# Where a tile starts in SBUF: widening four small tiles so that all large tiles start at the same residue modulo 256 bytes

## The chip, the cores and the metric

The kernel runs on one core of one Trainium2 chip. The metric is the device time of one execution in microseconds (us). The time before is 1183.08 us, the median of 3 runs (1182.72 to 1183.48). In what follows PE is the matrix engine (TensorE), PEld its weight loads, DVE the vector engine, ACT the scalar engine, POOL GpSimd, SP the queue that issues most DMAs.

## The reference

One decoder layer over a sequence of 1024 tokens of width 1024, all in float32: a gated linear recurrence (HGRN2) with 8 heads of 128, an output projection, and an MLP with a squared ReLU of hidden width 4096, each behind an RMSNorm.

```python
h = _rmsnorm(x, norm_mix)
q, f, i, g = split(h @ w_in, 4)                      # (1024 x 1024) @ (1024 x 4096)
log_f = logaddexp(log(lb), log1p(-lb) + log_sigmoid(f));  k = (1 - lb) * sigmoid(-f)
S_t = diag(f_t) S_{t-1} + k_t v_t^T;  o_t = S_t^T q_t     # per head, in chunks
mix = (rms(o) * out_norm * silu(g)) @ w_out
x = x + mix
a = relu(_rmsnorm(x, norm_mlp) @ w1)                 # 1024 x 4096
x = x + (a * a) @ w2
out = _rmsnorm(x, norm_final)
```

## The kernel before

Every large product is done in a split form: an operand is kept as a rounded part and a remainder (`t[:, 0]` and `t[:, 1]`, or two tiles `h` and `l`), and `split_mm` (lines 206 to 209) issues three matmuls for a product of 128 x 128 by 128 x 512: high by high (L207), high by low (L208), low by high (L209). The third argument after the weights is the moving operand, of 512 columns; the weights of 128 columns are loaded by PEld while the matmul before runs. There are 4,464 such matmuls. On top of that the products go by a Strassen-like scheme of 7 block products for 8, whose sums of blocks are `t1` to `t4` on the side of the activations and `s1` to `s4` on the side of the weights.

The stages on PE, by the profile's names for their results, with matmuls of 512 columns:

| stage | from, to (us) | moving operand | weights | matmuls |
|---|---|---|---|---|
| `pp`: first head, unsplit | 14, 72 | `h0B` | `w0`, `w1` | 192 |
| `pX`, `pY`, `pZ`: 7 heads, beside the scan's small matmuls | 72, 438 | `h0B` and `t4`, or `t1` to `t3` | `w2` to `w15` | 1176, 504 of them on `t1` to `t3` |
| `op`: output projection | 438, 549 | `wo` | `zh` | 384 |
| `pl`: first MLP block, unsplit | 549, 597 | `h1B` | `wa0` to `wd0` | 192 |
| `m1X`, `m1Y`, `m1Z`: rest of `h @ w1`, 49 products of 24 | 597, 868 | `h1B` and `t4`, or `t1` to `t3` | 5 pairs of slots in turn | 1176 |
| `m2X`, `m2Y`, `m2Z`: `(a*a) @ w2`, 56 products of 24 | 868, 1176 | the same 5 pairs of slots | 5 pairs of activation slots in turn | 1344 |

(In the profile `t1` to `t4` are all called `ht`.) In `m2` the roles are turned round: the activations are the weights of the matmul, and `w2` moves.

The order on PE is the program's own, and so it is on the other engines but for some of the work between the stages. While PE works on one product, ACT and DVE split the operands of a later one (L775 and L776 the weights, L944 and L945 the activations, L111 and L112 the sums `t`), and SP loads and stores the blocks.

SBUF is given out by pools. The pool `keep` (line 51) grows from the bottom: the identity, `gn`, `mk`, `neghalf` (line 67), then the slots `m0` to `m3`, then small tiles (`lb`, line 258, and others), then the slots `m4` to `m11` and the 16 slots `hT`, then small tiles again (`fs`, line 997, 12 buffers). The pools `scan` (to about 500 us) and `mlp` (after it) stand behind it. The pool `right` (line 53) grows down from the top and holds the 12 slots `d0` to `d11`. A tile takes its columns times 4 bytes in each partition, rounded up to 32. Nearly all slots are of 4,096 bytes, so within a run of slots all start at the same residue modulo 256, and which one is decided by the small tiles ahead of them:

| slots | start modulo 256 | what lies there |
|---|---|---|
| `m0` to `m3` | 32 | raw `w_in`, raw `w_out`; in `m1` and `m2` one of the 5 pairs of weight slots (`m2`, `m3`) and one of the 5 pairs of activation slots |
| `m4` to `m11`, `hT` | 192 | weights of `pp` and `p`; the other 4 pairs of weight slots; `h0B`, `h1B`, `t4`, `zh`, raw `w2` |
| pools `scan`, `mlp` | 128 | the scan's `q`, `k`, `f`, `v`; MLP results `e`, `t`; the other 4 pairs of activation slots |
| `d0` to `d11` | 224 | `x`, `t1` to `t3`, `wo`, `acc`, outputs |

Of the kernel before, what the change touches and what calls it, by code (L numbers as in the profile page):

```python
# [21 lines left out]
F32 = mybir.dt.float32  # L22
# [7 lines left out]
P = 128  # L30
# [18 lines left out]
def trunk(ctx: ExitStack, tc: tile.TileContext, x, gains, masks, gfin, w_in, w_out, w1, w2, out):  # L49
    nc = tc.nc  # L50
    pool = ctx.enter_context(tc.tile_pool(name="keep", bufs=1))
    dram = ctx.enter_context(tc.tile_pool(name="dram", bufs=1, space=bass.MemoryType.DRAM))
    dp = ctx.enter_context(tc.tile_pool(name="right", bufs=1, side="right"))
# [10 lines left out]
    make_identity(nc, ident)  # L64
    gn = pool.tile([P, 4, 8], F32, name="gn")
    mk = pool.tile([P, 8, LEAF], U8, name="mk")
    neghalf = pool.tile([P, 8], F32, name="neghalf")
    nc.gpsimd.memset(neghalf, -0.5)


# [4 lines left out]
    def hslot(half, kb, name):  # L75
        return pool.tile([P, 2, 512], F32R, name=name, tag=f"hT{half}{kb}")

    def dslot(i, shape, name, dt=F32):
        return dp.tile(shape, dt, name=name, tag=f"d{i}")
# [22 lines left out]
    def split_sum(n):  # L102
        half, k0 = SUMS[n]
        for kb in range(4):
            r = R[half, k0 + kb // 2][:, kb % 2]
            if n == "t4":
                t = hslot(1, kb, f"ht4{kb}")
            else:
                t = dslot(("t1", "t2", "t3").index(n) * 4 + kb, [P, 2, 512], f"h{n}{kb}", F32R)
            hc[n, kb] = t  # L110
            nc.scalar.activation(t[:, 0], r, AF.Copy)  # L111
            nc.vector.tensor_tensor(t[:, 1], r, t[:, 0].bitcast(F32), ALU.subtract)  # L112
# [132 lines left out]
    with tc.tile_pool(name="scan", bufs=1) as sp:  # L245
# [9 lines left out]
        Ac = sp.tile([P, NC, LEAF], F32, name="Ac")  # L255


        lb = pool.tile([P, 8], F32, name="lb")
        lo = pool.tile([P, 8], F32, name="lbe")
        nc.vector.tensor_tensor(lb, gn[:, 3, :], gn[:, 3, :], ALU.subtract)  # L260
        nc.scalar.activation(lb, lb, AF.Exp)
# [23 lines left out]
        def value(half, k):  # L285

            shape, name = [P, 2, 512], f"R{half}{k}"
            if (half, k) in ((0, 0), (0, 1), (1, 0)):
                return dslot(8 + 2 * half + k, shape, name)
            tag = {(1, 1): "AT", (0, 2): "kt", (0, 3): "S", (1, 2): "oz", (1, 3): "v"}[half, k]  # L290
            return sp.tile(shape, F32, name=name, tag=tag)
# [87 lines left out]
        def plain_pair(h, tl, j, half):  # L379

            for r in range(2):
                p_ = psum.tile([P, 512], F32, name=f"pp{h}{j}{half}{r}", tag="d")
                for k in range(2):
                    w = weight(2 * h + j, "abcd"[2 * r + k])
                    for kb in range(4):
                        hook()
                        t = hc[BLOCKS[half][k], kb]
                        c = slice(kb * P, (kb + 1) * P)
                        split_mm(p_, w[:, 0, c], w[:, 1, c], t[:, 0], t[:, 1], (k, kb) == (0, 0), (k, kb) == (1, 3))
                        if kb == 2 or (j, half, r, k) == (0, 0, 0, 0):  # L390
                            i = index[2 * h + j, "abcd"[2 * r + k]]
                            ensure(min(i + 3, 4 * PLAIN) if half == 0 else i + 4)
                        pump(650.0)
                if (j, r) == (0, 0):
                    q_part(h, tl, 512 * half, p_)
                elif j == 0:
                    f_half(h, tl, half, p_, 1.0)
                    f_bound(h, tl["f"][:, HALF[half]])
                elif r == 0:
                    tiles(h, tl, "vT")  # L400
                    nc.scalar.activation(tl["vT"][:, HALF[half]], p_, AF.Copy)
                else:
                    g_half(h, tl, half, p_, 1.0)
# [56 lines left out]
        def scan_units(h, tl):  # L460
# [60 lines left out]
            def leaf(m, i):  # L521
                def run():
# [8 lines left out]
                    if m == LEAF // 2:  # L531
                        for b in range(P // LEAF):
                            r = slice(b * LEAF, (b + 1) * LEAF)
                            nc.scalar.activation(AT[r, :, r], Ac[r, :, :], AF.Copy)  # L534
                return run
# [12 lines left out]
            def big(m):  # L548
                def run():
# [8 lines left out]
                    for s0 in range(0, P, 2 * m):  # L558
                        for par in range(2):
                            nc.scalar.activation(AT[s0:s0 + m, par::2, s0 + m:s0 + 2 * m],  # L560
                                                 ps[s0 + m * par:s0 + m * (par + 1)], AF.Copy)
# [42 lines left out]
            def o_unit():  # L604
# [4 lines left out]
                for g in range(2):  # L609
                    ps = psum.tile([P, 4, P], F32, name=f"o{h}{g}", tag="s")  # L610
                    st["o"].append(ps)
                    for j in range(4):
                        c = 4 * g + j
                        nc.tensor.matmul(ps[:, j, :], AT[:, c, :], v[:, c, :], start=True, stop=c == 0)  # L614
                        if c:
# [38 lines left out]
        block_sums()  # L654
        for n in ("t1", "t3", "t2"):
            split_sum(n)
        AT = sp.tile([P, NC, P], F32, name="AT", tag="AT")
        nc.gpsimd.memset(AT, 0.0)
        plain_pair(0, tl, 0, 1)
# [334 lines left out]
        nc.sync.dma_start(t, x1[tb])  # L994

    def fs(name):
        return pool.tile([P, 1], F32, name=name, tag="fs", bufs=12)

    def out_tile(tb):
        return dp.tile([P, D], F32, name=f"ot{tb}", tag=f"d{9 + tb % 3}")  # L1000
# [6 lines left out]
    def rows_out(tb):  # L1007
        ot, ss = out_tile(tb), fs(f"fs{tb}")
        nc.scalar.activation(ot, acc[tb], AF.Square, scale=D ** -0.5, accum_out=ss)  # L1009
        r = rstd_of(ss, EPS, 1, f"f{tb}")  # L1010
        nc.vector.scalar_tensor_tensor(ot, acc[tb], r[:, 0:1], gf, op0=ALU.mult, op1=ALU.mult)
        nc.sync.dma_start(out[tb * P:(tb + 1) * P, :], ot)

    def rows_first_half(tb):

        ot, ss = out_tile(tb), fs(f"fs{tb}")
        nc.scalar.activation(ot[:, :512], acc[tb][:, :512], AF.Square, scale=D ** -0.5, accum_out=ss)
        nc.gpsimd.tensor_scalar(ss, ss, EPS, None, op0=ALU.add)
        nc.vector.tensor_tensor(acc[tb][:, :512], acc[tb][:, :512], gf[:, :512], ALU.mult)
        small[tb] = ss  # L1020

    def rows_second_half(tb):
        ot, ss = out_tile(tb), fs(f"ft{tb}")
        nc.scalar.activation(ot[:, 512:], acc[tb][:, 512:], AF.Square, scale=D ** -0.5, accum_out=ss)
        r = fs(f"fr{tb}")
        nc.gpsimd.tensor_tensor(r, ss, small[tb], ALU.add)
        nc.gpsimd.tensor_tensor(r, r, neghalf[:, :1], ALU.pow)
        rows = slice(tb * P, (tb + 1) * P)
        nc.scalar.activation(ot[:, :512], acc[tb][:, :512], AF.Copy, scale=r[:, 0:1])
        nc.scalar.dma_start(out[rows, :512], ot[:, :512])  # L1030
        nc.vector.scalar_tensor_tensor(ot[:, 512:], acc[tb][:, 512:], r[:, 0:1], gf[:, 512:],
                                       op0=ALU.mult, op1=ALU.mult)
        nc.sync.dma_start(out[rows, 512:], ot[:, 512:])
# [109 lines left out]
```

## Time and profile before

| | before |
|---|---|
| median of 3 runs | 1183.08 us |
| the profiled execution, its own time | 1184.61 us |
| its span (first to last instruction) | 1182.8 us |
| mean granted PE clock | 0.991 |
| PE busy, share of the span | 1157.9 us, 98% |
| DVE, ACT, POOL busy | 797.6, 569.8, 70.7 us |
| DMA | 143.38 MB, mean 121 GB/s |

A busy PE says little by itself: a matmul of 512 columns is shown with about 390 ns, and the next one starts some 227 to 236 ns after it, so neighbours overlap. How fast PE goes is read from the starts: so many matmuls between two starts in the timeline.

### The profile page before, as it was taken

What the parts mean: (1) busy time and instruction counts of PE and PEld (TensorE: products, weight loads), DVE (VectorE), ACT (ScalarE), POOL (GpSimd) and SP (SyncE); (2) the same over time, 40 slices, a digit from 0 to 9 for tenths busy, and PEclk for the clock granted to TensorE, in tenths of its full rate; (3) what the DMA queues carried; (4) which work ended last, traced back from release to release, by engine and by line L of the source; (5) the groups of instructions that cost most, each with busy time, mean ns of one, the idle gap of its engine ahead of it and who ended that gap; (6) DMA issues with size and microseconds to landing.
All of it is one profiled execution on the core that took longest, in us unless ns stands there. A gap on an engine that the chain in (4) does not pass through costs nothing.

```text
span 1182.8 us, 17554 instructions
## 1 busy us (share of the span) xinstructions
PE 1157.9 (98%) x7108; PEld 947.9 (80%) x7108; DVE 797.6 (67%) x1131; ACT 569.8 (48%) x999; POOL 70.7 (6%) x94
## 2 busy tenths in 40 slices
PE   8989999999999999999999999999999999999997
PEld 7777788887878777888888888888888888888886
DVE  5897868787787867425846545654578756677663
ACT  7446455564645564236645444444453443323552
POOL 7500000000000000010000000000000000000011
PEclk9899999999999998999999999999999999999999
DMA  6111111111112175021245234523797544422331
GB/s 254 36 37 37 55 57 64 43 54 55 37 55 71 37 234 194 19 89 71 89 160 192 86 132 178 196 108 111 274 343 303 182 174 155 157 98 90 125 125 72
DMA packets 43138, 143.38 MB, mean 121 GB/s; under 512 B 4912, under 2 KB 5040, under 8 KB 43056
## 3 DMA queue, kind: packets, MB, share of 16 engines
q1 hardware_dynamic: 42192, 141.05, 33.7%
q8 instruction: 56, 0.92, 0.3%
q10 hardware_dynamic: 864, 1.20, 0.3%
q14 instruction: 26, 0.21, 0.1%
HBM read 100.81 MB, written 41.42 MB: 120 GB/s over the span
## 4 chain that ended last, share of the span: by engine, by line
PE 86%; DVE 8%; DMA 2%; POOL 2%; ACT 1%; issue 1%; SPq 0%; POOLq 0%; DVEq 0%; ACTq 0%
PE m2X L207 5%; PE m2X L209 5%; PE m2X L208 5%; PE m1X L207 4%; PE m1X L208 4%; PE m1X L209 4%; PE pX L207 3%; PE pX L208 3%; PE pX L209 3%; PE op L207 3%; PE op L208 2%; PE op L209 2%; PE m2Y L207 2%; PE m2Y L209 2%; PE m2Y L208 2%; PE m1Y L207 2%
## 5 line engine op out<-in xcount | busy, mean ns | idle before, releaser
L944 ACT ACTIVATE a<-ai 128x1024 fp32r<-128x1024 f32 x56 | 59.0, 1054 | 74.5 <-PE m2X L208 25.1
L945 DVE TENSOR_TENSOR a<-ai,a 128x1024 fp32r<-128x1024 f32 x56 | 68.3, 1219 | 11.8 <-ACT a L944 11.8
L847 ACT ACTIVATE e<-e 128x1024 f32<-128x1024 f32 x21 | 22.3, 1062 | 67.8 <-DVE e L978 67.8
L207 PE MATMUL op<-wo,zh 128*128 128x512 f32 x128 | 52.4, 409 | 0.0
L208 PE MATMUL op<-wo,zh 128*128 128x512 f32 x128 | 51.2, 400 | 0.0
L209 PE MATMUL op<-wo,zh 128*128 128x512 f32 x128 | 51.2, 400 | 0.0
L147 DVE TENSOR_TENSOR xr<-xr,op 128x512 f32<-128x512 f32 x24 | 16.5, 688 | 46.5 <-PE op L209 46.3
L1005 DVE TENSOR_TENSOR acc<-acc,m2X 128x512 f32<-128x512 f32 x32 | 21.2, 685 | 37.2 <-PE m2X L209 37.1
L321 DVE TENSOR_TENSOR q<-q,f 128x512 f32<-128x512 f32 x56 | 38.6, 689 | 3.8 <-PE lv L557 2.1
L328 DVE TENSOR_TENSOR k<-k,f 128x512 f32<-128x512 f32 x56 | 38.4, 686 | 0.1
L121 POOL TENSOR_SCALAR rs_f<-fs 128x1 f32<-128x1 f32 x4 | 2.1, 518 | 585.2 <-ACT ot L1009 585.2
L844 ACT ACTIVATE e<-e 128x1024 f32<-128x1024 f32 x32 | 34.0, 1062 | 1.0
L534 ACT ACTIVATE AT<-Ac 32x256 f32<-32x256 f32 x32 | 13.3, 415 | 33.7 <-DVE Ac L530 33.4
L147 DVE TENSOR_TENSOR raw<-raw,raw 128x512 f32<-128x512 f32 x42 | 28.9, 689 | 0.7
L209 PEld LDWEIGHTS op<-wo,zh 128*128 128x128 f32 x128 | 24.4, 191 | 6.0
L207 PEld LDWEIGHTS op<-wo,zh 128*128 128x128 f32 x128 | 24.5, 192 | 5.8
L208 PEld LDWEIGHTS op<-wo,zh 128*128 128x128 f32 x128 | 24.5, 191 | 5.5
L966 ACT ACTIVATE e<-m1X 128x512 f32<-128x512 f32 x28 | 16.0, 592 | 23.8 <-PE m1X L209 23.8
L121 POOL TENSOR_SCALAR rs_z<-zs 128x8 f32<-128x8 f32 x8 | 1.9, 243 | 402.3 <-ACT z L620 402.3
L300 POOL TENSOR_TENSOR R<-h0B 128x512 f32<-128x512 f32 x16 | 25.5, 1627 | 6.4 <-DVE h0B L297 6.4
L626 ACT ACTIVATE z<-o,rs_z 128x128 f32<-128x128 f32 x64 | 17.4, 384 | 16.4 <-POOL rs_z L122 16.4
L614 PE MATMUL o<-v,AT 128*128 128x128 f32 x128 | 23.4, 275 | 0.0
(1720 smaller groups left out, 3766.4 us busy)
## 6 DMA issues: line engine op xcount, KB each, us to landing
raw<-in_w_in SPq DMA_DIRECT2D x32, 512.0 KB, 3.7
ai<-adt SPq DMA_DIRECT2D x32, 512.0 KB, 4.3
adB<-e SPq DMA_DIRECT2D x24, 512.0 KB, 2.6
adt<-t SPq DMA_DIRECT2D x24, 512.0 KB, 4.6
ai<-adB SPq DMA_DIRECT2D x24, 512.0 KB, 4.5
x<-in_x SPq DMA_DIRECT2D x8, 512.0 KB, 7.3
xr<-in_x SPq DMA_DIRECT2D x8, 512.0 KB, 5.4
iw<-in_w_out SPq DMA_DIRECT2D x16, 256.0 KB, 3.4
```

Of the source, the lines that this page charges most:

```text
L147: nc.vector.tensor_tensor(out_, a, b, ALU.add)
L207: nc.tensor.matmul(ps, lhi, rhi, start=start, stop=False, **more)
L208: nc.tensor.matmul(ps, lhi, rlo, start=False, stop=False, **more)
L209: nc.tensor.matmul(ps, llo, rhi, start=False, stop=stop, **more)
L300: nc.gpsimd.tensor_tensor(R[half, kb // 2][:, kb % 2], t[:, 0].bitcast(F32), t[:, 1].bitcast(F32), ALU.add)
L321: nc.vector.tensor_tensor(qo, qo, te.to_broadcast([P, n, m]), ALU.mult)
L328: nc.vector.tensor_tensor(ke, ke, to.to_broadcast([P, n, m]), ALU.mult)
L614: nc.tensor.matmul(ps[:, j, :], AT[:, c, :], v[:, c, :], start=True, stop=c == 0)
L844: nc.scalar.activation(t, t, AF.Square)
L847: nc.scalar.activation(t, t, AF.Relu, scale=sign)
L944: nc.scalar.activation(hi, x, AF.Copy)
L945: nc.vector.tensor_tensor(lo, x, hi.bitcast(F32), ALU.subtract)
```

## The change

Three small tiles get wider or more buffers, and one that nothing reads or writes is added:

- `neghalf` from 8 to 48 columns (32 to 192 bytes): all that follows in `keep` moves up by 160 bytes, `m0` to `m3` from residue 32 to 192.
- `lb` from 8 to 32 columns, of which the first 8 are used (32 to 128 bytes): what follows moves up by 256 bytes in all, so `m4` to `m11` and `hT` stay at 192.
- `fs` from 12 to 14 buffers (64 bytes more): `scan` and `mlp` move up by 320 bytes in all, from 128 to 192.
- `edge`, 32 bytes in `right`: `d0` to `d11` move down by 32 bytes, from 224 to 192.

So every slot of 4 KB starts at 192 modulo 256, and so do the larger ones and those of 2,048 and 3,584 bytes. The program's instructions are the same on every engine and stand in the same order; the one that differs is the memset of `neghalf` on POOL, 48 columns for 8.

```diff
-    neghalf = pool.tile([P, 8], F32, name="neghalf")
+    neghalf = pool.tile([P, 48], F32, name="neghalf")
     nc.gpsimd.memset(neghalf, -0.5)
...
-        lb = pool.tile([P, 8], F32, name="lb")
+        lb = pool.tile([P, 32], F32, name="lb")[:, :8]
...
         for n in ("t1", "t3", "t2"):
             split_sum(n)
+        dp.tile([P, 8], F32, name="edge")
         AT = sp.tile([P, NC, P], F32, name="AT", tag="AT")
...
     def fs(name):
-        return pool.tile([P, 1], F32, name=name, tag="fs", bufs=12)
+        return pool.tile([P, 1], F32, name=name, tag="fs", bufs=14)
```

## Rows read from the trace of the kernel before

**Rows 1.** The page, part 1: busy us (share of the span) xinstructions.

```profile
PE 1157.9 (98%) x7108; PEld 947.9 (80%) x7108; DVE 797.6 (67%) x1131; ACT 569.8 (48%) x999; POOL 70.7 (6%) x94
```

**Rows 2.** The page, part 4: the chain that ended last, by engine.

```profile
PE 86%; DVE 8%; DMA 2%; POOL 2%; ACT 1%; issue 1%; SPq 0%; POOLq 0%; DVEq 0%; ACTq 0%
```

**Rows 3.** Busy time by stage: length, busy us (x instructions), PE clock, DMA share, GB/s.

```profile
72.00:438.00 366.00, 359.20 (x3361) 294.72 (x3350) 286.37 (x547) 198.95 (x493) 13.40 (x14) 1.00 0.20 64
438.00:549.00 111.00, 106.61 (x662) 86.81 (x661) 55.25 (x100) 40.31 (x87) 7.71 (x16) 0.97 0.29 102
597.00:868.00 271.00, 271.00 (x1177) 220.49 (x1176) 150.19 (x148) 132.01 (x158) 0.00 (x0) 1.00 0.44 167
868.00:1176.00 308.00, 307.86 (x1345) 252.07 (x1343) 214.05 (x213) 122.42 (x137) 10.18 (x18) 1.00 0.46 164
```

**Rows 4.** Timeline, PE, first matmuls of products: start us, us, engine, line, out<-moving,weights.

```profile
585.74 0.39 PE L207 MATMUL pl<-h1B,wc0h 128*128 128x512 f32 x1
...
602.06 0.40 PE L207 MATMUL m1Y<-ht,ws11h 128*128 128x512 f32 x1
...
607.66 0.39 PE L207 MATMUL m1X<-ht,ws21h 128*128 128x512 f32 x1
...
613.26 0.40 PE L207 MATMUL m1Y<-h1B,ws41h 128*128 128x512 f32 x1
```

**Rows 5.** Timeline, PE: two products that move `t4`, by two weight slots.

```profile
784.99 0.39 PE L207 MATMUL m1X<-ht,wd5h 128*128 128x512 f32 x1
...
790.43 0.39 PE L207 MATMUL m1X<-h1B,wa6h 128*128 128x512 f32 x1
...
823.63 0.39 PE L207 MATMUL m1X<-ht,wd6h 128*128 128x512 f32 x1
...
829.24 0.39 PE L207 MATMUL m1X<-h1B,wa7h 128*128 128x512 f32 x1
```

**Rows 6.** Timeline, PE: first and last of `m2`, and products in it.

```profile
867.88 0.39 PE L207 MATMUL m2X<-va0sh,a 128*128 128x512 f32 x1
...
1128.45 0.39 PE L208 MATMUL m2X<-vs37sl,a 128*128 128x512 f32 x1
...
1131.62 0.39 PE L207 MATMUL m2Z<-vb4sh,a 128*128 128x512 f32 x1
...
1142.62 0.39 PE L207 MATMUL m2Z<-vb6sh,a 128*128 128x512 f32 x1
...
1175.46 0.40 PE L209 MATMUL m2X<-vd7sh,a 128*128 128x512 f32 x1
```

**Rows 7.** Timeline, PE: a stretch of `op` without other work, and the wait in it.

```profile
445.51 1.51 PE L509 MATMUL lv<-qe,k 128*32 128x48 f32 x64 [4.38 <-ACT qe L502]
...
500.58 0.39 PE L207 MATMUL op<-wo,zh 128*128 128x512 f32 x1
...
528.58 0.39 PE L207 MATMUL op<-wo,zh 128*128 128x512 f32 x1
```

**Rows 8.** Timeline, PE: two products of the heads' stage.

```profile
120.59 0.39 PE L207 MATMUL pX<-ht,w3s 128*128 128x512 f32 x1
...
123.39 0.39 PE L207 MATMUL pY<-h0B,w3s 128*128 128x512 f32 x1
...
127.59 0.40 PE L207 MATMUL pX<-ht,w3d 128*128 128x512 f32 x1
...
130.32 0.39 PE L207 MATMUL pX<-h0B,w4a 128*128 128x512 f32 x1
```

**Rows 9.** Groups of elementwise work: shapes xcount | busy us, mean ns | idle before.

```profile
L147 DVE TENSOR_TENSOR vc<-vc,va 128x1024 f32<-128x1024 f32 x8 | 9.8, 1219 | 0.0
L856 DVE TENSOR_TENSOR t<-e,e 128x1024 f32<-128x1024 f32 x8 | 9.7, 1219 | 0.0
```

**Rows 10.** Timeline, ACT and DVE: the split of the weights `ws21`.

```profile
591.60 1.06 ACT L775 ACTIVATE ws21h<-uc 128x1024 fp32r<-128x1024 f32 x1 [2.55 <-DVE uc L147]
...
592.70 1.23 DVE L776 TENSOR_TENSOR ws21l<-uc,ws21h 128x1024 fp32r<-128x1024 f32 x1 [1.13 <-ACT ws21h L775]
```

## The prediction

> **What bounds the kernel now.** I read the page's busy times and its chain first: PE is busy for 98% of the span and holds 86% of the chain that ended last, DVE 8%, DMA 2% [rows 1, 2]. Then the stages: from 597 to 1176 us PE is busy without a gap (271.00 of 271.00 and 307.86 of 308.00 us), in the heads' stage it idles for 6.8 us of 366 and in the output projection for 4.4 of 111 [rows 3]. So in the MLP the time is the number of matmuls times the distance of their starts, and nothing else; before it this holds nearly, with waits between.
>
> That distance is no constant, and it goes by where the operands lie. I set the timeline's starts beside the table of residues:
>
> - moving operand and weights both at 192: 72 matmuls from 585.74 to 602.06, 16.32 us, 226.7 ns each [rows 4];
> - moving at 224 (`t1`, `t2`): 24 in 5.60 us, 233.3 ns, with the weights at 32 (`ws11`, from 602.06) as at 192 (`ws21`, from 607.66) [rows 4];
> - the same tile `t4` at 192 moving, in one place against weights at 192, in the other against weights at 32: 5.44 and 5.61 us for 24, or 226.7 and 233.8 ns [rows 5]. Stage, engines at work and moving operand are the same; the weight slot alone differs. This pair convinces me most;
> - in `m2`, moving at 192 and weights at 128: 48 from 1131.62 to 1142.62, 11.00 us, 229.2 ns [rows 6];
> - in `m2`, both at 32: the last 14 of a product, from 1128.45 to 1131.62, take 3.17 us, 226.4 ns [rows 6];
> - moving `wo` at 224, weights at 192: 120 in 28.00 us, 233.3 ns [rows 7].
>
> Equal residues run at 226.7 ns, whichever they are; unequal ones at 229 or 233 to 234.
>
> **The change, part by part.** It moves no instruction. It makes the residue of every operand 192, so each class above should go to the first one. I take 226.7 ns (5.44 us for a product of 24) as the pace after, and count stage by stage.
>
> `m2`: 1344 matmuls from 867.88 to 1175.46 us, that is 1343 distances in 307.58 us [rows 6]. At 226.67 ns they are 304.42 us: 3.16 us less. Against it: after a change of class the pace needs some ten matmuls to settle (the product at 32 reached its pace only in its last 14). With one class there is nothing to settle, but the stops of other kinds remain; I take 2.7. Bounds 0 (rival 4) and 3.16; for a loss see rival 3.
>
> `m1`: 49 products from 596.6 us (585.74 and 48 matmuls of `pl` at 226.7 ns) [rows 4, 6] to 867.88, so 271.3 us; 49 x 5.44 is 266.6. That is 4.7 us less, nearly all of it from 26 slow products (21 that move `t1` to `t3`, and 5 more with the weight slot at 32) at 0.16 to 0.17 us each. I take 4.4; bounds 0.8 (the 5 products alone) and 4.7.
>
> `pl`: two products of 24 have their weights at 32, 0.17 us each: 0.3 us.
>
> `op`: 384 matmuls, some 350 of them running free at 233.3 ns. 350 x 6.6 ns is 2.3 us. The stage also holds a wait of 4.38 us for data that the last head's scan and a DMA bring [rows 7]; what PE gains ahead of such a wait is given back in it. I take 2.0; bounds 0 and 2.3.
>
> Heads' stage: 42 products of 12 move `t1` to `t3` at 2.80 us, against 2.73 us for one that moves `t4` [rows 8]. The difference is 0.07 us, so 2.9 us in all. Here not everything is on PE's path: PE waits 6.8 us in all [rows 3], for the scan's DVE work, and DVE is busy 286 of 366 us, so a part of a faster PE turns into longer waits. I take half, 1.5; bounds 0 and 2.9.
>
> `pp`: all at 192 already, nothing.
>
> Elementwise work: a DVE addition of 1,024 columns takes 1219 ns with its tiles at 192 and 1219 ns with them at 128 [rows 9]. So DVE gains and loses nothing by the residue, and the cover it needs (it is busy 364 of the MLP's 579 us) is not touched. The longer memset of `neghalf` is 40 columns more, on POOL, long before the first use: nothing. The DMAs move the same bytes to the same slots, behind a PE that is the bound: nothing. If PE is 3% faster within a product, the splits for the next ones must be ready 0.17 us sooner; with DVE idle for a third of the MLP and PE waiting nowhere in it, I expect no new wait.
>
> Sum: 2.7 + 4.4 + 0.3 + 2.0 + 1.5 = 10.9 us. The profiled execution took 1184.61 us, 1.8 of it outside the span of 1182.8; the gain is all within the span, so 1173.7 for that execution, and from the median of 1183.08 I forecast **1172.2 us**.
>
> [...]
>
> **The rivals.**
>
> 1. *The upper pool is slow, not the residue.* All operands at 224 lie in `right`, at the top of SBUF, so place and residue can't be told apart for `t1` to `t3` and `wo`. If the place decides, `op` and the heads' stage gain nothing and `m1` only its 5 products: 0.8 + 2.7 + 0.3 = 3.8 us, 1179.3 us. For it: no tile in `right` has another residue. Against it: the slot at 32 lies low, among fast ones, and is as slow (233.8 against 233.3).
>
> 2. *The starts don't matter as such.* The weight slot at 32 is slow for another reason that the move does not cure (its distance to the moving tile in larger steps), and so is 224: 1183.1 us. Against it: the same slot at 32 is fast once the other operand is at 32 too [rows 6].
>
> 3. *Equal residues are fast only while the other engines keep away; slower.* After the change ACT, DVE and the DMAs work at 192 as well, where most of theirs now lies at 128 in the MLP. If each of their accesses at PE's residue costs PE its settled pace, the matmuls of `m1` and `m2` fall to 233.8 ns: 2519 x 0.2338 is 588.9 us for today's 578.9, 10 us more, and with half a microsecond from each stage ahead about 1194 us. It decides from a mean of 229.8 ns in the MLP, which is today's (578.9 us over 2519). Against it: while ACT and DVE write `ws21` into slots at 192 [rows 10], PE goes through the 72 matmuls at 226.7 ns without a flaw.
>
> 4. *`m2` doesn't settle.* The products with both at 32 spent their first ten matmuls at about 232 ns. If that is not the change of class but the way `m2` alternates two moving tiles, `m2` keeps its 229 ns: 1172.2 + 2.7 = 1174.9 us.
>
> **How the numbers follow.** The forecast has 0.62, rival 4 0.14, rival 1 0.11, rival 2 0.08, rival 3 0.05. All upper bounds together are 3.16 + 4.7 + 0.3 + 2.3 + 2.9 = 13.4 us, or 1169.7; I set the low end at 1169.5. The forecast's own lower end, with nothing from the heads' stage and half of `m2`, is about 8 us, 1175; to leave out no more than 2 in 10 the range goes on to rival 1's neighbourhood, 1179.5. A change of under 0.2% (2.4 us) can't be told from none in this kernel. Faster by more than that: the forecast, rival 4 and nearly all of rival 1, 0.86. Within it: rival 2 and the rest of rival 1, 0.09. Slower: 0.05.
>
> **What would show it.** In the profile after, a product of `m1` that moves `t1` takes 5.44 us and no longer 5.60, one with the weights in slots `m2` and `m3` the same, `m2` lasts 304 to 305 us, `op` shows 226.7 ns in its free stretch, and the waits in the heads' stage grow by about as much as is missing there. DVE's 1219 ns stays. The forecast is wrong if `t1` keeps 233 ns at 192 (rival 1), if `m2` stays at 229 (rival 4), if the products with slots `m2` and `m3` stay slow (rival 2), or if those that were settled at 226.7 ns lose that pace (rival 3).

## The result, and the profile after

The changed kernel takes **1172.06 us** (median of 6 runs, 1170.51 to 1175.24) against 1183.17 (6 runs, 1182.72 to 1183.53): a ratio of 0.9905, 95% interval 0.9894 to 0.9916. The profiled execution took 1173.07 us with a span of 1171.2, against 1184.61 and 1182.8. Two lines went in, so line numbers after are one or two higher (the matmuls are at L208 to L210).

The page after, part 1 (busy us), the chain by engine, and two rows of part 6 (KB, us to landing):

```profile
PE 1145.7 (98%) x7108; PEld 948.1 (81%) x7108; DVE 796.5 (68%) x1131; ACT 569.1 (49%) x999; POOL 68.5 (6%) x94
...
PE 85%; DVE 8%; DMA 2%; ACT 2%; POOL 1%; issue 1%; SPq 0%; POOLq 0%; DVEq 0%; ACTq 0%
...
ai<-adt SPq DMA_DIRECT2D x32, 512.0 KB, 4.4
...
va<-in_w SPq DMA_DIRECT2D x8, 512.0 KB, 6.1
```

The instructions are as many as in [rows 1]; PE is busy for 12.2 us less, the other engines for about the same. The bound has not moved: PE is at 98% as before and holds nearly the same share of the chain [rows 2]. Busy time by stage after, with the columns of [rows 3]:

```profile
72.00:437.00 365.00, 358.14 (x3331) 295.44 (x3331) 286.10 (x547) 198.00 (x492) 13.38 (x14) 1.00 0.21 65
437.00:545.00 108.00, 102.72 (x652) 85.23 (x651) 54.72 (x100) 39.41 (x86) 7.69 (x16) 0.97 0.29 102
593.00:859.00 266.00, 266.00 (x1176) 220.24 (x1175) 149.50 (x147) 131.33 (x157) 0.00 (x0) 1.00 0.45 169
859.00:1165.00 306.00, 305.25 (x1347) 252.44 (x1345) 214.70 (x213) 122.84 (x138) 8.39 (x18) 1.00 0.47 167
```

In `m1` PE goes through 1176 matmuls in 266.00 us where it had 1177 in 271.00, still without a gap and at the same granted clock of 1.00. In `m2` the last 0.75 us of the window is past the last matmul. PE is not freed of a wait; it goes faster. The timeline of PE after shows where (start us, us, line, out<-moving,weights):

```profile
119.60 0.39 PE L208 MATMUL pX<-ht,w3s 128*128 128x512 f32 x1
...
122.32 0.39 PE L208 MATMUL pY<-h0B,w3s 128*128 128x512 f32 x1
...
443.88 1.51 PE L510 MATMUL lv<-qe,k 128*32 128x48 f32 x64 [5.28 <-ACT qe L503]
...
495.54 0.39 PE L208 MATMUL op<-wo,zh 128*128 128x512 f32 x1
...
522.74 0.39 PE L208 MATMUL op<-wo,zh 128*128 128x512 f32 x1
...
582.01 0.39 PE L208 MATMUL pl<-h1B,wc0h 128*128 128x512 f32 x1
...
598.33 0.39 PE L208 MATMUL m1Y<-ht,ws11h 128*128 128x512 f32 x1
...
603.77 0.39 PE L208 MATMUL m1X<-ht,ws21h 128*128 128x512 f32 x1
...
609.21 0.39 PE L208 MATMUL m1Y<-h1B,ws41h 128*128 128x512 f32 x1
...
815.93 0.39 PE L208 MATMUL m1X<-ht,wd6h 128*128 128x512 f32 x1
...
821.37 0.39 PE L208 MATMUL m1X<-h1B,wa7h 128*128 128x512 f32 x1
...
859.45 0.39 PE L208 MATMUL m2X<-va0sh,a 128*128 128x512 f32 x1
...
1118.07 0.39 PE L209 MATMUL m2X<-vs37sl,a 128*128 128x512 f32 x1
...
1120.57 0.39 PE L208 MATMUL m2Z<-vb4sh,a 128*128 128x512 f32 x1
...
1131.45 0.39 PE L208 MATMUL m2Z<-vb6sh,a 128*128 128x512 f32 x1
...
1163.86 0.39 PE L210 MATMUL m2X<-vd7sh,a 128*128 128x512 f32 x1
```

- The 72 matmuls from 582.01 that were fast before are as fast: 16.32 us [rows 4].
- `ws11` and `ws21`, which move `t1` and `t2` from the upper pool, take 5.44 us each, no longer 5.60 [rows 4].
- `t4` against `wd6`, whose slot has moved from 32 to 192, takes 5.44 us, no longer 5.61 [rows 5].
- `m2`: 1343 distances from 859.45 to 1163.86 are 304.41 us, 226.67 ns each, for 307.58 [rows 6]; 48 from 1120.57 take 10.88 us for 11.00.
- The free stretch of `op`: 120 in 27.20 us for 28.00, but the wait ahead of `lv` is 5.28 us for 4.38 [rows 7].
- A product of twelve with `t1` in the heads' stage: 2.72 us for 2.80 [rows 8].

Of the 2520 matmuls of `m1` and `m2` not one starts other than 226 or 227 ns after its forerunner. The products that the prediction had settling over ten matmuls settle no more, since nothing changes class.

Elementwise work after, the counterparts of [rows 9] (shapes xcount | busy us, mean ns | idle before):

```profile
L148 DVE TENSOR_TENSOR vc<-vc,va 128x1024 f32<-128x1024 f32 x8 | 9.7, 1218 | 0.0
L858 DVE TENSOR_TENSOR t<-e,e 128x1024 f32<-128x1024 f32 x8 | 9.7, 1218 | 0.0
```

`vc` and `va` lie at 192 as before; `t` and `e` have moved from 128 to 192, and their addition takes 1218 ns for 1219.

From the starts of each stage's first matmul of 512 columns, the length of every stage in us (start: up to the first such matmul; tail: past the last):

| kernel | start | pp | heads | op | pl | m1 | m2 | tail | span |
|---|---|---|---|---|---|---|---|---|---|
| before | 13.89 | 58.62 | 365.65 | 110.64 | 47.82 | 271.26 | 307.57 | 7.37 | 1182.8 |
| after | 15.36 | 56.45 | 363.90 | 109.58 | 47.59 | 266.56 | 304.41 | 7.36 | 1171.2 |
| e1_right | 15.14 | 56.59 | 363.72 | 107.98 | 47.81 | 268.56 | 307.57 | 7.36 | 1174.7 |
| e2_slots | 14.41 | 58.67 | 367.00 | 110.51 | 47.62 | 270.48 | 306.81 | 7.35 | 1182.8 |
| e3_fs14 | 15.47 | 56.58 | 365.91 | 110.08 | 47.79 | 271.27 | 305.71 | 7.36 | 1180.2 |
| e4_fs13 | 14.45 | 58.65 | 364.54 | 110.08 | 47.81 | 271.27 | 312.22 | 7.36 | 1186.4 |
| e5_all224 | 15.36 | 56.56 | 363.92 | 107.78 | 47.62 | 266.56 | 304.41 | 7.34 | 1169.6 |
| e6_right64 | 14.35 | 58.46 | 365.84 | 110.95 | 47.59 | 270.01 | 304.41 | 7.36 | 1179.0 |
| e7_right128 | 14.38 | 58.51 | 365.87 | 110.21 | 47.59 | 270.20 | 304.41 | 7.36 | 1178.5 |
| e8_right0 | 14.24 | 58.37 | 364.92 | 107.48 | 47.59 | 268.61 | 304.41 | 7.29 | 1172.9 |
| e9_all0 | 13.92 | 58.42 | 363.54 | 107.57 | 47.61 | 266.56 | 304.41 | 7.28 | 1169.3 |
| e10_no_edge | 14.05 | 58.40 | 365.92 | 110.03 | 47.60 | 270.48 | 304.41 | 7.35 | 1178.2 |

`m1` and `m2`, where PE never waits, repeat to 0.01 us and follow the residues alone. `start` and `pp` together lie between 71.7 and 73.1 us whatever the residues.

### The profile page after: what moved, and what is told of

Same layout as the page of the kernel before. It is cut to its first block, busy times and chain, and to the rows that moved or that the text cites. A ratio compares the mean times of both kernels' runs of the same rounds, so it can differ in the third digit from the quotient of the medians.

```text
span 1171.2 us, 17554 instructions
## 1 busy us (share of the span) xinstructions
PE 1145.7 (98%) x7108; PEld 948.1 (81%) x7108; DVE 796.5 (68%) x1131; ACT 569.1 (49%) x999; POOL 68.5 (6%) x94
## 4 chain that ended last, share of the span: by engine, by line
PE 85%; DVE 8%; DMA 2%; ACT 2%; POOL 1%; issue 1%; SPq 0%; POOLq 0%; DVEq 0%; ACTq 0%
PE m2X L210 5%; PE m2X L209 5%; PE m2X L208 5%; PE m1X L208 4%; PE m1X L209 4%; PE m1X L210 4%; PE pX L208 3%; PE pX L210 3%; PE pX L209 3%; PE op L208 3%; PE m2Y L210 2%; PE m2Y L209 2%; PE m2Y L208 2%; PE op L210 2%; PE op L209 2%; PE m1Y L208 2%
## 5 line engine op out<-in xcount | busy, mean ns | idle before, releaser
L947 DVE TENSOR_TENSOR a<-ai,a 128x1024 fp32r<-128x1024 f32 x56 | 68.3, 1219 | 11.3 <-ACT a L946 11.3
L208 PE MATMUL op<-wo,zh 128*128 128x512 f32 x128 | 51.8, 405 | 0.0
L210 PE MATMUL op<-wo,zh 128*128 128x512 f32 x128 | 50.7, 396 | 0.0
L210 PEld LDWEIGHTS op<-wo,zh 128*128 128x128 f32 x128 | 24.4, 191 | 5.4
L208 PEld LDWEIGHTS op<-wo,zh 128*128 128x128 f32 x128 | 24.6, 192 | 5.1
```

What stands on the lines that cost most here:

```text
L208: nc.tensor.matmul(ps, lhi, rhi, start=start, stop=False, **more)
L210: nc.tensor.matmul(ps, llo, rhi, start=False, stop=stop, **more)
L947: nc.vector.tensor_tensor(lo, x, hi.bitcast(F32), ALU.subtract)
```

## The experiments

The theory: the pace of a matmul goes by the difference of the starts of its two operands, moving minus weights, modulo 256 bytes; 0 is the fastest. The rivals on record were that the upper pool as a place is slow, that starts don't matter as such, and that PE's gain depends on what the other engines do; later ones were that a start has a value of its own, and that the period is another. Each experiment changes nothing but the widths of small tiles. The ratios are to the kernel before as it ran beside each experiment: 1183.81 us for e1 to e4, 1184.46 for the others.

**e1_right**: the kernel before with only the upper pool moved, 224 to 192.

```diff
+        dp.tile([P, 8], F32, name="edge")
```

> The upper pool alone moves, from 224 to 192 (x, t1 to t3, wo, acc, outputs); all else as before. Theory 1, the pace of a matmul goes by the difference between the starts of its moving operand and its weights modulo 256, 0 being fast (226.7 ns): in m1 the 16 products that move t1 to t3 against weights at 192 fall from 5.60 to 5.44 us (2.6 us), the 5 against weights at 32 stay at about 5.60; op and the heads' stage gain what they gained in the full change, 1.05 and 1.75 us. Sum about 5.5 us, 1177.6 us. Theory 2, every operand that starts off a multiple of 64 bytes costs by itself: the same here. Rival, the gain of the full change is of the MLP pools and slots alone: no change, 1183.2 us.

Measured: 1176.84 us, ratio 0.9950 (0.9932 to 0.9968). PE's timeline of this kernel:

```profile
596.68 0.39 PE L207 MATMUL m1Y<-ht,ws11h 128*128 128x512 f32 x1
...
602.30 0.39 PE L207 MATMUL m1X<-ht,ws21h 128*128 128x512 f32 x1
...
607.76 0.39 PE L207 MATMUL m1Y<-h1B,ws41h 128*128 128x512 f32 x1
```

`ws21`, now 192 against 192, takes 5.46 us; `ws11`, whose weights are still at 32, stays at 5.62. The upper pool is not slow as a place, and moving one operand helps only where the other one is there already.

**e2_slots**: the kernel before with only the slots `m0` to `m3` moved, 32 to 192.

```diff
-    neghalf = pool.tile([P, 8], F32, name="neghalf")
+    neghalf = pool.tile([P, 48], F32, name="neghalf")
...
-        lb = pool.tile([P, 8], F32, name="lb")
+        lb = pool.tile([P, 32], F32, name="lb")[:, :8]
```

> Only the slots m0 to m3 move, from 32 to 192; the upper pool stays at 224, scan and mlp at 128. Theory 1: in m1 the 5 products that move h1B or t4 against these slots gain 0.17 us each, the 5 that move t1 to t3 stay slow (224 against 192), two products of pl gain 0.3 us; in m2 the 11 products with both at 32 go to both at 192 and lose nothing but their own settling (0.05 us each). Sum 0.85 + 0.3 + 0.5 = 1.7 us, 1181.5 us. Theory 2: the same for m1 and pl, 0.5 to 1 us more in m2. Rival: nothing, 1183.2 us.

Measured: 1182.11 us, ratio 0.9987 (0.9976 to 0.9999). PE's timeline of this kernel:

```profile
603.64 0.40 PE L207 MATMUL m1Y<-ht,ws11h 128*128 128x512 f32 x1
...
609.24 0.39 PE L207 MATMUL m1X<-ht,ws21h 128*128 128x512 f32 x1
...
614.84 0.40 PE L207 MATMUL m1Y<-h1B,ws41h 128*128 128x512 f32 x1
```

Both products stay at 5.60 us: `ws11` got the weight residue of the fast class and gained nothing, since its moving operand is at 224. `m1` gains 0.78 us, about 0.16 for each of the five products that move a tile at 192 against the slots that were at 32.

**e3_fs14** and **e4_fs13**: the kernel before with only `scan` and `mlp` moved, from 128 to 192 and to 160. They carry the weights of most of `m2`.

```diff
-        return pool.tile([P, 1], F32, name=name, tag="fs", bufs=12)
+        return pool.tile([P, 1], F32, name=name, tag="fs", bufs=14)
```

(e4: `bufs=13`.)

> Only the pools scan and mlp move, from 128 to 192. Theory 1: the 45 products of m2 with moving at 192 and weights at 128 go from 5.49 to 5.44 us, but for some unsettled matmuls behind each product with both at 32: 2.2 us, 1181.0 us; m1, op and the heads' stage as before. Theory 2: 128 and 192 are both multiples of 64, so nothing, 1183.2 us.

> The pools scan and mlp move by 32 bytes only, from 128 to 160. One more buffer for a tile of 4 bytes should make the kernel slower. Theory 1: the 45 products of m2 with moving at 192 and weights at 160 go from 5.49 to some 5.61 us, 5 us more: 1188.3 us, slower by 0.4%. Theory 2: the same for another reason (160 is no multiple of 64). Rival, nothing in m2 depends on the start: 1183.2 us.

Measured: e3 1182.02 us, ratio 0.9988 (0.9977 to 1.0000); e4 1188.14 us, ratio 1.0041 (1.0025 to 1.0057), so slower by 0.4%. PE's timeline, first and last matmul of `m2`, of e3:

```profile
867.10 0.39 PE L207 MATMUL m2X<-va0sh,a 128*128 128x512 f32 x1
...
1172.81 0.39 PE L209 MATMUL m2X<-vd7sh,a 128*128 128x512 f32 x1
```

and of e4:

```profile
866.80 0.39 PE L207 MATMUL m2X<-va0sh,a 128*128 128x512 f32 x1
...
1179.02 0.39 PE L209 MATMUL m2X<-vd7sh,a 128*128 128x512 f32 x1
```

The same 1344 matmuls last 305.71 us with the weights of 45 of the 56 products at 192, 307.57 with them at 128 and 312.22 at 160, or 227.6, 229.0 and 232.5 ns on average; the other 11 products have both operands at 32 in all three. Nearest in distance is not nearest in time: a difference of 32 costs more than one of 64. In e3 the two operands are equal in every product of `m2`, but the products at 32 still alternate with those at 192, and each alternation costs the settling, 1.30 us in all; only when everything lies at one residue does `m2` reach 304.41 (e10_no_edge). The intervals of e2 and e3 end at 1 or next to it, so what these two show rests on the stages and not on the total.

**e5_all224**: the kernel before with everything moved to 224, where the upper pool lies already.

```diff
-    neghalf = pool.tile([P, 8], F32, name="neghalf")
+    neghalf = pool.tile([P, 56], F32, name="neghalf")
...
-        lb = pool.tile([P, 8], F32, name="lb")
+        lb = pool.tile([P, 32], F32, name="lb")[:, :8]
...
-        return pool.tile([P, 1], F32, name=name, tag="fs", bufs=12)
+        return pool.tile([P, 1], F32, name=name, tag="fs", bufs=14)
```

> All slots at one residue again, but at 224, no multiple of 64. Theory 1 (the difference decides): all matmuls of the MLP at 226.7 ns, the time of the full change, about 1172 us. Theory 2 (each operand off a multiple of 64 costs by itself): m1 and m2 at 233 ns and more, 2520 x 6.7 ns = 17 us slower than the full change, and op and the heads' stage as before, about 1192 us.

Measured: 1171.93 us, ratio 0.9894 (0.9882 to 0.9907). PE's timeline of this kernel:

```profile
596.70 0.39 PE L207 MATMUL m1Y<-ht,ws11h 128*128 128x512 f32 x1
...
602.13 0.39 PE L207 MATMUL m1X<-ht,ws21h 128*128 128x512 f32 x1
...
857.81 0.39 PE L207 MATMUL m2X<-va0sh,a 128*128 128x512 f32 x1
...
1162.23 0.39 PE L209 MATMUL m2X<-vd7sh,a 128*128 128x512 f32 x1
```

At 224 the matmuls go exactly as at 192. 224 is not bad and 192 not good: equality decides. This settles it against every theory of one operand's start.

**e6_right64**, **e7_right128** and **e8_right0**: the changed kernel with `edge` 40, 24 and 56 columns wide, so that the upper pool lies at 64, 128 and 0 and all else stays at 192.

```diff
-        dp.tile([P, 8], F32, name="edge")
+        dp.tile([P, 40], F32, name="edge")
```

> The full change, but the upper pool at 64 instead of 192: t1 to t3 and wo move at 64 against weights at 192, a difference of 128. If the period is 128 bytes, the difference is none: 226.7 ns, about 1172 us. If it is 256, a third pace, somewhere between 229 and 234 ns: the 21 products of m1 that move t1 to t3 take 5.50 to 5.61 us, op and the heads' stage lose with them, 1174 to 1178 us. Theory 2: 64 is a multiple of 64, so 226.7 ns, 1172 us.

> The full change, but the upper pool at 128: moving at 128 against weights at 192, a difference of 192 modulo 256, the one that 224 against 32 had before (233.4 ns). Theory 1 with period 256: 233 ns in the 21 products of m1 (5.60 us each, 3.4 us), op and heads as before (2.8 us): about 1178 us. If the difference counts without its sign, it is 64, as 192 against 128 had in m2 (229 ns): about 1174 us. Theory 2: 1172 us.

> The full change, but the upper pool at 0: moving at 0 against weights at 192, a difference of 64 modulo 256, the one that 192 against 128 had in m2 before (229 ns). Theory 1 with period 256: 229 ns in the 21 products of m1 (5.50 us), a third of the loss: about 1174 us. A rival that wants the moving operand at a start of 256 bytes: 226.7 ns or less, 1172 us or below.

Measured: 1180.02 us, ratio 0.9958 (0.9944 to 0.9972); 1180.32, 0.9957 (0.9944 to 0.9971); 1176.48, 0.9932 (0.9919 to 0.9945). PE's timeline from `ws11` to `ws21` of e6:

```profile
602.62 0.39 PE L208 MATMUL m1Y<-ht,ws11h 128*128 128x512 f32 x1
...
608.21 0.40 PE L208 MATMUL m1X<-ht,ws21h 128*128 128x512 f32 x1
```

of e7:

```profile
602.00 0.39 PE L208 MATMUL m1Y<-ht,ws11h 128*128 128x512 f32 x1
...
607.60 0.39 PE L208 MATMUL m1X<-ht,ws21h 128*128 128x512 f32 x1
```

and of e8, `ws21`:

```profile
603.56 0.39 PE L208 MATMUL m1X<-ht,ws21h 128*128 128x512 f32 x1
...
609.05 0.40 PE L208 MATMUL m1Y<-h1B,ws41h 128*128 128x512 f32 x1
```

24 matmuls take 5.59, 5.60 and 5.49 us: 233, 233 and 229 ns. The difference of 128 (e6) is as slow as the rest, so the period is not 128. Nor is it 512: by the layout of the changed kernel `m2` and `m3` start at 192 modulo 512 and the upper pool at 448, which is 256 apart, and `ws11`, which pairs the two, takes 5.44 us there. That of 192 (e7) is slow, that of 64 (e8, 0 minus 192) is the middle class of `m2` before, with another pair of residues: so the sign counts. All three took some 2 us more than expected. Against after, the span of e6 is 7.8 us longer: 3.45 in `m1`, 1.94 in the heads' stage, 1.37 in `op`, and 1.0 in `start` and `pp`, which do not go by the residues; with these last taken off, the rest is what the slow pairs give.

**e9_all0**: everything at 0, equal and on a multiple of 256.

```diff
-    neghalf = pool.tile([P, 48], F32, name="neghalf")
+    neghalf = pool.tile([P, 64], F32, name="neghalf")
...
-        dp.tile([P, 8], F32, name="edge")
+        dp.tile([P, 56], F32, name="edge")
```

> As the changed kernel, but every slot of 4 KB starts at 0 modulo 256 bytes (neghalf 64 columns, edge 56), so all are equal and aligned to 256 bytes. Theory 1 (PE's pace goes by the difference of the two operands' starts and nothing else in this kernel does): m1 266.6 us, m2 304.4 us, DMA and elementwise durations as before, time 1171 to 1173 us, no difference from the changed kernel. Rival (an aligned start also helps the DMAs, which carry 164 GB/s in the MLP, or another engine): PE waits nowhere in the MLP, so a gain can show only in the waits of the heads' stage and of op and in the start of some 14 us: 1168 to 1171 us, and a lower median time from issue to landing. Rival 2 (a start at a multiple of 256 collides with something else): m1 and m2 above 226.7 ns a matmul, over 1175 us.

Measured: 1171.16 us, ratio 0.9895 (0.9881 to 0.9908). PE's timeline of this kernel:

```profile
596.49 0.39 PE L208 MATMUL m1Y<-ht,ws11h 128*128 128x512 f32 x1
...
601.93 0.39 PE L208 MATMUL m1X<-ht,ws21h 128*128 128x512 f32 x1
...
857.61 0.39 PE L208 MATMUL m2X<-va0sh,a 128*128 128x512 f32 x1
...
1162.03 0.39 PE L210 MATMUL m2X<-vd7sh,a 128*128 128x512 f32 x1
```

and two of its DMA rows:

```profile
ai<-adt SPq DMA_DIRECT2D x32, 512.0 KB, 4.4
...
va<-in_w SPq DMA_DIRECT2D x8, 512.0 KB, 6.4
```

The matmuls are those of after, and the transfers land as late (4.4 for 4.4 us, 6.4 for 6.1): no row here shows a gain from the aligned start. The intervals of after, e5 and e9 overlap almost wholly: all three are one kernel in time, and none beats the changed one by what can be measured.

**e10_no_edge**: the changed kernel without `edge`, so with the upper pool at 224.

```diff
-        dp.tile([P, 8], F32, name="edge")
```

> The changed kernel without the tile edge: the upper pool stays at 224, all else at 192. Theory 1 (pairs alone decide, so the parts add): m2 stays at 304.4 us, m1 keeps 21 products at 233.3 ns and lasts 266.6 + 21 x 0.16 = 269.9 us, op goes at 233.3 ns, the heads' stage keeps its 42 slower products: the changed kernel's 1172.1 plus 3.4 plus about 1 for op plus about 1.8 for the heads, 1178 to 1179 us; the parts measured alone (a wider edge 7.0 us, the low slots 1.1, fs 1.8 gained) sum to 9.9 of the 11.1 us. Rival (the gain came from the upper pool's place being moved at all, or the parts need one another): 1180.3 or more, m2 above 305 us.

Measured: 1179.67 us, ratio 0.9962 (0.9948 to 0.9976). PE's timeline of this kernel:

```profile
601.44 0.40 PE L208 MATMUL m1Y<-ht,ws11h 128*128 128x512 f32 x1
...
607.04 0.39 PE L208 MATMUL m1X<-ht,ws21h 128*128 128x512 f32 x1
...
866.48 0.39 PE L208 MATMUL m2X<-va0sh,a 128*128 128x512 f32 x1
...
1170.89 0.39 PE L210 MATMUL m2X<-vd7sh,a 128*128 128x512 f32 x1
```

`m2` has its whole gain without `edge` (304.41 us), `ws11` none (5.60 us), and the median lies 0.7 us above my range. The parts do not add up to the whole: in `m1`, e1, e2 and e3 gain 2.70, 0.78 and nothing, 3.48 together, and the change 4.70. Five products move a tile of the upper pool against slots that were at 32; they are slow until both are moved, which is 5 x 0.16 = 0.8 us. The other 0.4 us I put to the settling that goes when the last class is gone; this part is argued and not measured by itself. (The 9.9 us in the expectation took the low slots' 1.1 us against another median of the kernel before; against the 1183.81 us beside them they gained 1.7, and the three parts 10.5.)

## Why the prediction was right, and where its steps were off

The forecast was 1172.2 us for 1172.06. The mechanism was right: the instructions and transfers are the same, and PE's pace changed where the residues did. The sum of 10.9 us came out at 11.6 in the span (11.5 in the execution's own time, 11.1 between the medians), and its terms were these:

| term | taken | bounds | measured |
|---|---|---|---|
| `m2` | 2.7 | 0 to 3.16 | 3.16 |
| `m1` | 4.4 | 0.8 to 4.7 | 4.70 |
| `pl` | 0.3 | - | 0.23 |
| `op` | 2.0 | 0 to 2.3 | 1.06 |
| heads' stage | 1.5 | 0 to 2.9 | 1.75 |
| start and `pp` | 0 | - | 0.70 |

That the total comes within 0.2 us is in part luck: `m2`, `m1`, the heads' stage and the start came out 1.71 us above what was taken, `op` and `pl` 1.01 below, and the medians lie 0.4 us closer together than the two profiled executions.

- **`m2` and `m1`** reached their upper bounds to the hundredth. What I kept back for stops of other kinds was not needed: with one class the pace is reached once, and PE holds it for 571 us. Rival 4 (`m2` alternates two moving tiles and can't settle) fell.
- **`op`** was over-sized. Its free matmuls gave about 2.0 us of the 2.3 that I had counted (353 in 82.37 us before, 352 in 80.15 after). But the wait grew from 4.38 to 5.28 us and took 0.9 back, which I had named and not priced. This can't be put to the change: over the twelve profiles the wait lies between 3.80 us (e8) and 5.41 (e6) whatever the pairs, and in e9, with all pairs as equal as after, it is 4.32; in e1, e5, e8 and e9 the stage lasts 107.5 to 108.0 us. Behind the wait the starts of some eight matmuls are 427 ns apart (granted clock 0.72 from 440 to 452 us), before as after, so this explains none of the difference. What is certain is the free pace.
- **The heads' stage** was nearly the right size for a wrong reason. I had expected half of the gain to turn into longer waits of PE; it did not. PE idles 6.86 us of 365.00 in that stage after, against 6.80 of 366.00 [rows 3]. The other half was never there: 29 products of twelve (`t1` to `t4`) run unbroken, and they went from 82.93 to 81.14 us; the others are cut into 54 pieces of 3 to 9 matmuls by other work of PE, and went from 84.98 to 84.64. The starts within these pieces are 247 ns apart on average in the kernel before, for `t4` at 192 as for `t1` to `t3` at 224: the first distance of a piece is 305 ns on average and the second 232 (303 and 231 after), and 21 of the 54 pieces end there, with three matmuls. And of the 1.79 us of the unbroken ones 0.44 lies in the first product, 4.44 us before and 4.00 after, and hardly comes from the residues: behind a wait of 3.07 us before and 3.02 after, seven of its distances are about 427 ns before and four after (granted clock 0.56 and 0.68 from 82.00 to 85.50 us). The other 28 gave 1.35 us, or 0.064 for each of the 21 among them that move `t1` to `t3`, close to the 0.07 forecast.
- **Start and `pp`**, forecast at nothing, shrank by 0.70 us. Over the twelve profiles the two together vary by 1.4 us without regard to the residues, so this is not put to the change.
- **Rival 1** (the upper pool is slow) fell by e1, e5 and the changed kernel itself. **Rival 2** (starts don't matter as such) fell by e4: 32 bytes in the place of `scan` and `mlp` alone cost 4.65 us in `m2`. **Rival 3** (the other engines' work at 192 spoils PE) fell: the mean in the MLP is 226.67 ns, with ACT, DVE and the DMAs as busy as before.

In the MLP after, no other engine is seen to slow PE (226 or 227 ns throughout). The two operands of a matmul do bear on each other: at one and the same granted clock of 1.00, the relative start alone adds 6.6 ns to 226.7 (moving at 224 against weights at 192, in `m1` before).

What stays open: why. The traces show a pace for a pair of starts, not what lies behind it. Differences of 96 and 224 bytes, and steps finer than 32, were not run.

## What to carry to other kernels

Where PE is the bound and its matmuls run back to back, list the start addresses of both operands modulo 256 bytes and the distance of the starts in the timeline beside them; if the distance goes by the pair, pad small tiles until both operands of every hot product have the same residue, and the same one from product to product (alternating between two cost 1.30 us in `m2` of e3). Do it for all pools at once, as a pair gains only when both of its sides are there (`ws11` stays at 5.62 us in e1 and at 5.60 in e2), and look again after any edit that adds a few bytes ahead of the big tiles: one more small buffer (e4) cost 0.4%. Here it paid in long unbroken rows of matmuls (7.86 us in `m1` and `m2`) and hardly at all where other work cuts them short (0.34 us in the pieces of the heads' stage). All of this is shown for one form of matmul alone, 128 x 128 weights loaded anew for each 512 columns.

## What the runs showed of the hardware that was not expected

Distance of the starts of 512-column matmuls at a granted clock of 1.00, by the difference of the starts, moving minus weights, modulo 256 bytes. Each figure is the mean over the matmuls of `m1` or `m2` past the twelfth after a change of the pair:

| difference | ns | pairs (moving, weights) |
|---|---|---|
| 0 | 226.7 | 192, 192 (after); 32, 32 (before, `m2`); 224, 224 (e5); 0, 0 (e9) |
| 64 | 228.9 | 192, 128 (before, `m2`); 0, 192 (e8) |
| 32 | 233.3 | 192, 160 (e4); 224, 192 (before, `m1`) |
| 128 | 233.5 | 64, 192 (e6) |
| 160 | 234.0 | 192, 32 (before, `m1`) |
| 192 | 233.3 to 233.5 | 128, 192 (e7); 224, 32 (before, `m1`) |

The loss does not grow with the difference, and it depends on its sign (64 against 192). The figure at 64 is a mean of three: the starts are about 232, 226 and 229 ns apart in turn, one step for each of the three matmuls of a split product, in `m2` of the kernel before as in e8; after, at 0, all three are 226 or 227. DVE's additions of 1,024 columns show nothing of the kind: `t<-e,e` takes 1219 ns before, with its tiles at 128, and 1218 after, with them at 192.
